# One level of Strassen's scheme in the MLP's up projection of a hybrid encoder layer (24 of 32 inner tiles), its results carried through DRAM

## The chip, the cores and the metric

The kernel runs on one core of a Trainium2 chip, in one launch. The metric is the device time of one execution in microseconds (us), from the first to the last instruction and what lies around them; the time stated for a kernel is the median of its runs. The core's engines run beside each other: TensorE (PE) multiplies, VectorE (DVE), ScalarE (ACT) and GpSimd (POOL) work element by element, SyncE (SP) issues every DMA of this kernel.

## The reference, cut to what matters

One layer of a streaming encoder, for 1024 prompt frames and 32 new frames that share the weights (1056 tokens, model width 1024, all float32). After a windowed attention, a short convolution and a memory cross attention comes the part that is changed:

```
hm = rms_norm(x, g_mlp)
x = x + jnp.square(jax.nn.relu(hm @ w_up)) @ w_down      # w_up 1024 x 4096, w_down 4096 x 1024
y = rms_norm(x, norm_final_g)
```

## The kernel before, in words

**Layout and precision.** Activations lie with features in the 128 partitions and tokens along the free axis. The tokens are cut into three chunks, `CH`: chunks 0 and 1 of 384 tokens, chunk 2 of 288. A width of 1024 is 8 feature tiles. Every operand of a large product is kept in two float32r parts, hi (a rounded copy, made by ACT) and lo (the rest, made by a subtraction), and `gemm` adds three matmuls for each of the 8 contraction tiles: hi by hi, hi weight by lo activation, lo weight by hi activation. One output tile of 128 features by one chunk is thus 24 matmuls of 384 or 288 columns, accumulated in one PSUM tile (`acc`, three buffers).

**Weights.** A weight tile is 128 by 1024: all 8 contraction tiles of 128 output features. `fetch_w` loads it (SP) into `wr` (two buffers), `issue_w` splits it into `wh` and `wl` (three buffers each). The split costs one ACT copy and one DVE subtraction; for the tiles that `shared` names (those of the phase with the cross attention) GpSimd makes the last 384 columns of `wl`. `next_w` keeps up to three tiles ready (`LOOK`).

**Order.** The program is a list, `plan`, of products with the weight tiles they need. From it a list scheduler fixes the order on each engine at build time: an instruction that is written later may stand earlier on its engine's queue where what it needs is ready by the scheduler's own clock. On the chip each queue runs in that fixed order.

**The phase around the change.** Chunk by chunk `trunk(c)` makes the convolution's output and the mixing product. The cross attention of chunk c, `cross_steps(c)`, is spread in 16 steps between the products of what follows: that of chunk 0 between those of `trunk(1)`, that of chunk 1 between those of `trunk(2)`, that of chunk 2 between the first products of the MLP. Its last steps are `do_co(c, 0)` and `do_co(c, 1)`, which add the result to the residual `x1[c][f]`, scale it by the norm's gain and split it into `xm[c][f]` (`gain_split`), and `chunk_stats(c)`, which makes the norm's factor `R[c]` for each token. The factor is not multiplied into `xm`; `up_part` multiplies the product by it.

**The MLP.** The 4096 inner features are 32 tiles j in four groups of 8. Group 0 goes up one chunk at a time (its 8 weight tiles are loaded three times), so that chunk 0 can start while chunk 2's attention is still at work. After that: `do_down` of group 0 (8 output tiles, three chunks each), `do_up` of group 1, `do_down` of group 1, and so on. `up_part` takes a PSUM tile through DVE (maximum with 0, times `R`), squares it on GpSimd and on ACT, and splits the square into `hid[c][j]`, which stays in SBUF (pools `mpool`, `hx`, `hpool`) for the down products. The last group goes down chunk by chunk (`do_last`), with the final norm of a chunk beside the next one's products.

Of the kernel before, what the change touches and what calls it, by code (L numbers as in the profile page):

```python
# [27 lines left out]
NHX = 6  # L28

# Columns of the parameter block.  # L30
# [9 lines left out]
def hybrid_step(ctx: ExitStack, tc: tile.TileContext, io):  # L40
# [38 lines left out]
    ao_d, bc_d, m1_d = spill("ao_d"), spill("bc_d"), spill("m1_d")  # L79
    mk_d = dram.tile([2, P, 256], F32, name="mk_d")  # L80
# [20 lines left out]

    LOOK = 2
    ready = []
# [34 lines left out]
    def next_w(key):  # L138
        while len(ready) <= LOOK and wpos[0] < len(worder):
            issue_w()  # L140
        k, w = ready.pop(0)
        assert k == key, (k, key)
        return w
# [6 lines left out]
    def gemm(out, w, acts):  # L150
        """out[m, n] = sum over k of w[k][:, m] . acts[k], operands in two parts."""
# [7 lines left out]
    def gemm_tok(a, ws, acts, cols):  # L159
        """a[tokens, 256] from a block of 128 tokens and a [1024, 256] weight in two tiles."""  # L160
# [8 lines left out]
    # ------------------------------------------------------------------ norms  # L169
# [4 lines left out]
    def stats_col(accs, blocks, rcol):  # L174
        """rcol[:, j] = rsqrt(mean + eps) of token block j, from partitions' sums of squares."""
# [14 lines left out]
    def stats_row(blocks, n, rcol):  # L190
        """rcol's values along the free axis, in every partition (in PSUM)."""
# [40 lines left out]
    # =========================================== input norm; memory keys, values  # L232
# [9 lines left out]
    def norm_x():  # L242
# [31 lines left out]
        def squares(c):  # L274
            """Two partial sums of squares, each on an engine of its own."""
# [92 lines left out]
    # ============================== phase 1: windowed attention, short convolution  # L368
# [13 lines left out]
    def vtile(src):  # L382
        """[v in two parts, per head] from float32 values."""
# [492 lines left out]
    def do_co(c, half):  # L876
        def fn(w):
# [3 lines left out]
            for f in fs:  # L881
# [9 lines left out]
                if half == 0:  # L891
                    xm[c][f] = gain_split(x, G_MLP + f, c)
# [11 lines left out]
    def hslot(c):  # L904
        n = CH[c][1]
        if c == 0:
            return mslot(n)
# [260 lines left out]
```

## Time and profile before

| | |
|---|---|
| runs before | 1844.49, 1844.90, 1846.09 us; median 1844.9 us |
| the profiled execution | span 1844.3 us from first to last instruction |
| instructions | 29362, of them 11508 matmuls |
| DMA | 163.26 MB, mean 89 GB/s |

The profile's page gives for each engine its busy time, the span in 40 slices, the chain of work that ended last, and groups of like instructions with their mean duration and the idle time before them. Busy times of matmuls overlap, since they are pipelined; how fast TensorE works is read from the distance between the starts of neighbouring matmuls in the timeline. Idle time of an engine counts only where TensorE waits for it.

### The profile page before, as it was taken

How to read it: one execution, taken by the hardware profiler on the slowest of the kernel's cores; microseconds unless marked ns; L12 is line 12 of the kernel's file. 1: busy time of each engine (PE TensorE's matmuls, PEld its weight loads, DVE VectorE, ACT ScalarE, POOL GpSimd, SP SyncE). 2: the span in 40 equal slices, each digit the busy share in tenths (PEclk: the TensorE clock that was granted, in tenths of full speed). 3: DMA queues.
4: the chain of work that ended last, by engine and by line, in shares of the span. 5: the costliest groups of instructions: out<-in, count | busy, mean ns of one | idle time of the engine just before them, and what ended most of it. 6: DMA issues, size and time to landing. Idle time of an engine off the chain costs nothing.

```text
span 1844.3 us, 29362 instructions
## 1 busy us (share of the span) xinstructions
PE 1816.0 (98%) x11508; PEld 1801.8 (98%) x11508; DVE 994.9 (54%) x1919; ACT 669.2 (36%) x1342; POOL 403.1 (22%) x441
## 2 busy tenths in 40 slices
PE   7999999999999999999999999999999999999997
PEld 7999999999999999999999899999999999999997
DVE  7766767757664223336788988622332233223355
ACT  7643435435344102324566766401210121012234
POOL 3211010201100000026656664400210021002132
PEclk9999999999999999999999999999999999999999
DMA  4411111212123124225444443411111111111244
GB/s 176 140 64 59 62 55 59 70 56 70 56 93 107 58 94 150 76 83 189 163 137 153 143 135 98 137 46 42 43 46 45 46 45 46 46 46 47 69 147 142
DMA packets 72747, 163.26 MB, mean 89 GB/s; under 512 B 8961, under 2 KB 41889, under 8 KB 72481
## 3 DMA queue, kind: packets, MB, share of 16 engines
q1 hardware_dynamic: 72608, 161.38, 26.7%
q8 instruction: 91, 1.49, 0.3%
q14 instruction: 48, 0.39, 0.1%
HBM read 142.66 MB, written 18.69 MB: 87 GB/s over the span
## 4 chain that ended last, share of the span: by engine, by line
PE 89%; DVE 3%; DMA 3%; issue 2%; ACT 2%; POOL 1%; SPq 0%; POOLq 0%; ACTq 0%; DVEq 0%
PE acc L155 27%; PE acc L156 27%; PE acc L157 27%; PE pt L524 1%; PE sc L499 1%; DVE wl L132 1%; PE sc L498 1%; PE o L537 1%; PE o L536 1%; ACT wh L130 1%; DMA ct<-m_d 1%; DMA mkr<-mk_d 1%; POOL wl L134 1%; PE acc L165 0%; DVE Y L230 0%
## 5 line engine op out<-in xcount | busy, mean ns | idle before, releaser
L130 ACT CAST wh<-wr 128x1024 fp32r<-128x1024 f32 x220 | 230.9, 1050 | 579.6 <-PE acc L156 508.7
L155 PE MATMUL acc<-X,wh 128*128 128x384 f32 (+1 forms) x1200 | 390.8, 326 | 8.5 <-ACT wh L130 8.0
L156 PE MATMUL acc<-X,wh 128*128 128x384 f32 (+1 forms) x1200 | 387.8, 323 | 2.4 <-DVE X L230 2.4
L155 PE MATMUL acc<-Y,wh 128*128 128x384 f32 (+1 forms) x1200 | 388.4, 324 | 0.5 <-DVE Ga L890 0.2
L156 PE MATMUL acc<-Y,wh 128*128 128x384 f32 (+1 forms) x1200 | 388.0, 323 | 0.0
L157 PE MATMUL acc<-Y,wl 128*128 128x384 f32 (+1 forms) x1200 | 387.6, 323 | 0.0
L157 PE MATMUL acc<-X,wl 128*128 128x384 f32 (+1 forms) x1200 | 386.8, 322 | 0.3 <-DVE wl L132 0.3
L132 DVE TENSOR_TENSOR wl<-wr,wh 128x1024 fp32r<-128x1024 f32 (+1 forms) x220 | 263.8, 1199 | 79.7 <-ACT wh L130 78.2
L155 PEld LDWEIGHTS acc<-X,wh 128*128 128x128 f32 x1200 | 226.3, 189 | 9.2 <-ACT wh L130 8.0
L156 PEld LDWEIGHTS acc<-X,wh 128*128 128x128 f32 x1200 | 226.5, 189 | 4.1 <-DVE X L230 3.6
L157 PEld LDWEIGHTS acc<-X,wl 128*128 128x128 f32 x1200 | 226.2, 189 | 0.8 <-DVE wl L132 0.8
L155 PEld LDWEIGHTS acc<-Y,wh 128*128 128x128 f32 x1200 | 225.3, 188 | 1.2 <-DVE Ga L890 0.4
L156 PEld LDWEIGHTS acc<-Y,wh 128*128 128x128 f32 x1200 | 225.2, 188 | 0.0
L157 PEld LDWEIGHTS acc<-Y,wl 128*128 128x128 f32 x1200 | 225.1, 188 | 0.0
L925 POOL TENSOR_TENSOR ct<-ct 128x384 f32<-128x384 f32 (+1 forms) x96 | 77.7, 810 | 542.0 <-DVE ct L923 535.8
L134 POOL TENSOR_TENSOR wl<-wr,wh 128x384 fp32r<-128x384 f32 x84 | 118.4, 1410 | 315.9 <-ACT wh L130 314.9
L155 PE MATMUL acc<-M,wh 128*128 128x384 f32 (+1 forms) x448 | 148.1, 331 | 1.7 <-ACT M L107 1.4
L156 PE MATMUL acc<-M,wh 128*128 128x384 f32 (+1 forms) x448 | 147.6, 329 | 0.0
L157 PE MATMUL acc<-M,wl 128*128 128x384 f32 (+1 forms) x448 | 147.4, 329 | 0.0
L155 PE MATMUL acc<-H,wh 128*128 128x288 f32 (+1 forms) x416 | 129.2, 311 | 0.0
L157 PE MATMUL acc<-H,wl 128*128 128x288 f32 (+1 forms) x416 | 128.9, 310 | 0.0
L156 PE MATMUL acc<-H,wh 128*128 128x288 f32 (+1 forms) x416 | 128.9, 310 | 0.0
(235 smaller groups left out, 2727.1 us busy)
## 6 DMA issues: line engine op xcount, KB each, us to landing
wr<-in_w_in SPq DMA_DIRECT2D x50, 512.0 KB, 3.3
wr<-in_w_up SPq DMA_DIRECT2D x48, 512.0 KB, 3.3
wr<-in_w_down SPq DMA_DIRECT2D x48, 512.0 KB, 3.4
wr<-in_w_conv_out SPq DMA_DIRECT2D x24, 512.0 KB, 3.4
wr<-in_w_mix SPq DMA_DIRECT2D x24, 512.0 KB, 3.4
ao_d<-AO SPq DMA_DIRECT2D x32, 128.0 KB, 1.8
wr<-in_w_attn_out SPq DMA_DIRECT2D x8, 512.0 KB, 3.3
raw<-in_x SPq DMA_DIRECT2D x8, 384.0 KB, 6.1
```

The source lines that it names most:

```text
L130: act.copy(hi, raw)
L132: dve.tensor_sub(lo[:, :cut], raw[:, :cut], hi[:, :cut].bitcast(F32))
L134: pool_e.tensor_tensor(lo[:, cut:], raw[:, cut:], hi[:, cut:].bitcast(F32), op=ALU.subtract)
L155: pe.matmul(out, wh[:, a], hi, start=(k == 0), stop=False)
L156: pe.matmul(out, wh[:, a], lo, start=False, stop=False)
L157: pe.matmul(out, wl[:, a], hi, start=False, stop=(k == len(acts) - 1))
L498: pe.matmul(sc[:, h, j * w : j * w + w], q[h], a, start=True, stop=False)
L499: pe.matmul(sc[:, h, j * w : j * w + w], q[h], b, start=False, stop=True)
L524: pe.transpose(pt[:, h * P : h * P + P], self.stl[:, h, t * P : t * P + P], ident)
L536: pe.matmul(of, v, ph, start=(t == 0), stop=False)
L537: pe.matmul(of, v, pl, start=False, stop=(t == len(self.parts) - 1))
L925: pool_e.tensor_tensor(s, t, t, op=ALU.mult)
```

## The change: what it does

A pair of inner tiles (ja, jb), the two halves of the contraction (tiles 0 to 3 and 4 to 7) and chunks 0 and 1 form a 2 by 2 block product: weights A11, A12 (tile ja, halves 1 and 2) and A21, A22 (tile jb), activations B11, B21 (chunk 0, the two halves) and B12, B22 (chunk 1). Written out it takes 8 block products of 12 matmuls; by one level of Strassen's scheme (Winograd's form) it takes 7, with sums of weights (`s31`, `s24`) and differences of activations (`N1`, `N3`, `T2`, `N4`) as operands and a few additions on the results. Groups 1 to 3 (24 tiles, 12 pairs) are done in this way; group 0 and all of chunk 2 stay written out.

- The two chunks must have their norm's factor before the differences are taken. `normed_split` multiplies `x1` by gain and `R`, stores the result to DRAM (`xn_d`) and splits it; it stands after `chunk_stats(c)`, and `do_co` no longer splits for chunks 0 and 1.
- `combine(k)` loads four tiles of `xn_d` back and makes and splits the four differences of contraction tile k. The four `combine` calls and the weights of the first pair stand between the 8 products of `up0(2)`, group 0 of chunk 2.
- All up products now come before all down products. A finished square goes to DRAM (`hid_d`) unsplit; `load_hidden` loads and splits it for the down products, one group ahead. Group 0 goes down chunk 0 first, then chunks 1 and 2, so that its 8 weight tiles are loaded twice.
- The pool `hx` is gone; `late`, which lives during the up products, holds 8 working tiles `lt`, the second weight tile of a pair and its sums.

```diff
@@ do_co
-                if half == 0:
+                if half == 0 and c == 2:
                     xm[c][f] = gain_split(x, G_MLP + f, c)
@@ the MLP's pieces
+    def normed_split(c, f):
+        t = tmp(CH[c][1])
+        dve.scalar_tensor_tensor(t, x1[c][f], col(G_MLP + f), R[c], op0=ALU.mult, op1=ALU.mult)
+        sp.dma_start(xn_d[c][:, f], t)
+        xm[c][f] = (yslot(c), yslot(c))
+        split(*xm[c][f], t)
     def up_part(w, c, j):
         n = CH[c][1]
-        a = acc_tile([P, n])
-        gemm(a, w, xm[c])
+        a = ps.tile([P, n], F32, tag="pt", bufs=2, name=nm("pa")) if w[0] == "late" else acc_tile([P, n])
+        gemm(a, w[-2:], xm[c])
         t = tmp(n)
-        dve.scalar_tensor_tensor(t, a, 0.0, R[c], op0=ALU.max, op1=ALU.mult)
-        s = tmp(n)
-        pool_e.tensor_tensor(s, t, t, op=ALU.mult)
-        hi, lo = hslot(c), hslot(c)
-        act.activation(hi, t, AF.Square)
-        dve.tensor_sub(lo, s, hi.bitcast(F32))
-        hid[c][j] = (hi, lo)
+        if c == 2:
+            dve.scalar_tensor_tensor(t, a, 0.0, R[c], op0=ALU.max, op1=ALU.mult)
+        else:
+            dve.tensor_scalar_max(t, a, 0.0)
+        h = tmp(n)
+        pool_e.tensor_tensor(h, t, t, op=ALU.mult)
+        hidden(c, j, h)
+    def combine(k):
+        b11, b12, b21, b22, n1, n3, t2, n4 = (lt() for _ in range(8))
+        for t, c, f in ((b12, 1, k), (b22, 1, k + 4), (b11, 0, k), (b21, 0, k + 4)):
+            sp.dma_start(t, xn_d[c][:, f])
+        dve.tensor_sub(n3, b12, b22)
+        pool_e.tensor_tensor(n1, b11, b12, op=ALU.subtract)
+        dve.tensor_sub(t2, b11, n3)
+        pool_e.tensor_tensor(n4, b21, t2, op=ALU.subtract)
+        for kind, x in (("T2", t2), ("N1", n1), ("N3", n3), ("N4", n4)):
+            hi, lo = comb[kind, k] = (comb_slot(kind, k), comb_slot(kind, k))
+            act.copy(hi, x)
+            if kind[0] == "T":
+                dve.tensor_sub(lo, x, hi.bitcast(F32))
+            else:
+                pool_e.tensor_tensor(lo, x, hi.bitcast(F32), op=ALU.subtract)
+    def pair_issue(key, which):
+        r1, r2 = raws[key][:2]
+        a, b = slice(0, 512), slice(512, 1024)
+        if which == 4:
+            s31 = L["pool"].tile([P, 1024], F32, tag="s31", name=nm("s31"))
+            s24 = L["pool"].tile([P, 1024], F32, tag="s24", name=nm("s24"))
+            pool_e.tensor_tensor(s31[:, b], r2[:, a], r2[:, b], op=ALU.add)
+            pool_e.tensor_tensor(s24[:, a], r1[:, a], s31[:, b], op=ALU.add)
+            pool_e.tensor_tensor(s24[:, b], r1[:, b], s24[:, a], op=ALU.add)
+            pool_e.tensor_tensor(s31[:, a], r1[:, a], r2[:, a], op=ALU.add)
+            raws[key] += [s31, s24]
...
+        split(hi, lo, raws[key][src])
+    def up_pair(i, after):
...
+        up_fetch(i + 1)
+        A, B, C = (acc_tile([P, 384]) for _ in range(3))
+        product(A, w(1), 0, b11, True)
+        s1 = lt()
+        act.copy(s1, A)
+        product(B, w(4), 0, t2, True)
+        u2 = lt()
+        dve.tensor_sub(u2, B, s1)
+        product(A, w(1), 1, b21, False)
+        r, h = lt(), lt()
+        act.activation(r, A, AF.Relu)
+        pool_e.tensor_tensor(h, r, r, op=ALU.mult)
+        hidden(0, ja, h)
+        product(C, w(3), 1, n1, True)
+        product(B, w(3), 0, n3, False)
+        u3 = lt()
+        dve.tensor_sub(u3, B, s1)
+        v = lt()
+        dve.tensor_sub(v, u3, C)
+        square_relu(v, 1, jb)
+        up_part(("late", *w(1)), 2, ja)
+        up_issue(i + 1, 1)
+        product(C, w(4), 1, b22, False)
+        up_issue(i + 1, 4)
+        v = lt()
+        dve.tensor_sub(v, C, u2)
+        square_relu(v, 1, ja)
+        product(B, w(2), 1, n4, False)
+        up_issue(i + 1, 3)
+        v = lt()
+        dve.tensor_sub(v, B, s1)
+        square_relu(v, 0, jb)
+        up_part(("late", *w(2)), 2, jb)
+        up_issue(i + 1, 2)
+    def load_hidden(into, g, c, k):
+        t = tmp(n)
+        sp.dma_start(t, hid_d[c][:, 8 * g + k])
...
+        split(hi, lo, t)
@@ the order
-    left = beside(left + cross_steps(2), up0(0) + up0(1) + up0(2))
+    left = beside(left + cross_steps(2), up0(0) + up0(1))
+    for j in range(NF):
+        item(*do_up(j, 2))
+        if j < 4:
+            item(lambda j=j: combine(j))
+        if j == 4:
+            item(lambda: up_fetch(0))
+        if j == 5:
+            item(lambda: up_issue(0, 1))
+        if j == 6:
+            item(lambda: [up_issue(0, 4), up_issue(0, 2)])
+    item(lambda: up_issue(0, 3))
+    for i in range(len(UP)):
+        item(lambda i=i: up_pair(i, first_loads if i == len(UP) - 1 else lambda what: None))
+    item(open_down)
+    item(lambda: [load_hidden(nxt, 0, c, k) for c in (1, 2) for k in range(NF)])
-    for g in range(4):
-        if g:
-            for j in range(NF):
-                item(*do_up(g, j, range(3)))
-        if g < 3:
+    for g in range(3):
+        item(turn_group)
+        for cs, more in (([0], []), ([1, 2], range(3))) if g == 0 else ((range(3), range(3)),):
             for f in range(NF):
-                item(do_down(f), ("w_down", g, f))
+                item(do_down(g, f, cs, more), ("w_down", g, f))
```

In this diff `hidden(c, j, h)` stores `h` to `hid_d[c]`; `product` is 12 matmuls (4 contraction tiles, 3 each); `which` 1, 2, 3, 4 stands for the tiles `r1`, `r2` (split into `wh2`, `wl2`), `s31` and `s24`; `square_relu` makes max(v, 0) times v on DVE and stores it. In the last pair `first_loads` loads and splits group 0 of chunk 0 as the first two products free their operands' places.

More of the change, by code (lines that the diff above doesn't have):

```diff
@@ new lines, in product @@
+    def product(acc, w, half, acts, start):
+        wh, wl = w
+        for k, (hi, lo) in enumerate(acts):
+            a = slice(512 * half + k * P, 512 * half + k * P + P)
+            pe.matmul(acc, wh[:, a], hi, start=(start and k == 0), stop=False, skip_group_check=True)
+            pe.matmul(acc, wh[:, a], lo, start=False, stop=False, skip_group_check=True)
+            pe.matmul(acc, wl[:, a], hi, start=False, stop=(k == 3), skip_group_check=True)
+    UP = [(8 * g + i, 8 * g + i + 4) for g in range(1, 4) for i in range(4)]
@@ L969, in cross_steps @@
         steps.append(("call", [lambda: chunk_stats(c)]))
+        if c < 2:
+            steps[-1][1].extend(lambda f=f: normed_split(c, f) for f in range(NF))
         return steps
@@ L987, in trunk @@
         ]
-    up0 = lambda c: [do_up(0, j, [c]) for j in range(NF)]
+    up0 = lambda c: [do_up(j, c) for j in range(NF)]
     first = len(worder)
```

113 lines of the change are left out of this document (86 added, 27 removed).

## The prediction

> **What bounds the kernel now.** I read the page first: the busy shares and the chain of work that ended last.
>
> ```profile
> span 1844.3 us, 29362 instructions
> ## 1 busy us (share of the span) xinstructions
> PE 1816.0 (98%) x11508; PEld 1801.8 (98%) x11508; DVE 994.9 (54%) x1919; ACT 669.2 (36%) x1342; POOL 403.1 (22%) x441
> ...
> PE 89%; DVE 3%; DMA 3%; issue 2%; ACT 2%; POOL 1%; SPq 0%; POOLq 0%; ACTq 0%; DVEq 0%
> ```
>
> TensorE is busy 98% of the span and is 89% of the chain, so taking matmuls away should take time away, unless their place is filled by waiting. Whether it is filled is a question of stages, so I cut the stretch that the change touches into windows. In each row: length, then busy time of PE, weight loads, DVE, ACT, POOL.
>
> ```profile
> 945.00:985.00 40.00, 39.12 (x236) 37.95 (x235) 36.05 (x47) 25.39 (x40) 33.34 (x27) 1.00 0.38 128
> 985.00:1045.00 60.00, 58.97 (x424) 58.01 (x423) 53.12 (x101) 38.79 (x83) 33.20 (x30) 1.00 0.50 165
> 1045.00:1060.00 15.00, 12.96 (x79) 11.80 (x78) 13.48 (x19) 11.09 (x20) 13.39 (x13) 1.00 0.36 118
> 1060.00:1157.60 97.60, 96.01 (x608) 95.10 (x608) 84.94 (x146) 59.92 (x128) 56.64 (x48) 1.00 0.36 117
> 1157.60:1183.30 25.70, 25.61 (x193) 25.37 (x192) 20.00 (x35) 13.16 (x21) 15.12 (x14) 1.00 0.49 162
> 1183.30:1831.00 647.70, 647.70 (x4036) 647.70 (x4035) 227.43 (x346) 123.13 (x183) 83.79 (x93) 1.00 0.19 62
> ```
>
> The first three rows are cross attention of chunks 0 and 1, the fourth that of chunk 2 beside `up0(0)` and `up0(1)`, the fifth `up0(2)`, the last the rest of the MLP. In the last TensorE is never idle and DVE is at 227 of 648 us: room for everything. In the rows before it DVE runs at 78 to 90% and TensorE already loses a little (2.0 us in the third row). So the gain is made where there is room, and the preparation is put where there is little.
>
> **The gain.** The price of a matmul is the distance of starts, here across one output tile of 384 columns and one of 288:
>
> ```profile
> 1186.21 0.33 PE L157 MATMUL acc<-M,wl 128*128 128x384 f32 x1
> ...
> 1190.54 0.29 PE L155 MATMUL acc<-H,wh 128*128 128x288 f32 x1
> ...
> 1193.74 0.34 PE L155 MATMUL acc<-M,wh 128*128 128x384 f32 x1
> ```
>
> There are 25 steps of 384 columns in 4.33 us, 0.1732 us each, and 24 of 288 in 3.20 us, 0.1333 each. A pair took 2 tiles x 2 chunks x 24 = 96 matmuls of 384 columns and takes 7 x 12 = 84; chunk 2's 48 stay. 12 pairs x 12 = 144 matmuls, x 0.1732 = **24.9 us gained**. A pair lasts 84 x 0.1732 + 48 x 0.1333 = 20.9 us, a product of 12 lasts 2.1 us, a tile of chunk 2 lasts 3.2 us.
>
> **Inside the pairs.** These rows price what is added:
>
> ```profile
> L130 ACT CAST wh<-wr 128x1024 fp32r<-128x1024 f32 x220 | 230.9, 1050 | 579.6 <-PE acc L156 508.7 <-issue 45.1 <-DMA wr<-in_w_down 7.1
> L132 DVE TENSOR_TENSOR wl<-wr,wh 128x1024 fp32r<-128x1024 f32 x2 | 2.5, 1271 | 2.0 <-ACT wh L130 2.0
> L938 DVE TENSOR_TENSOR Gb<-acc,Gb 128x384 f32<-128x384 f32 x40 | 22.3, 557 | 97.5 <-PE acc L157 97.5
> L923 DVE SCALAR_TENSOR_TENSOR ct<-acc,R 128x288 f32<-128x288 f32 x8 | 3.4, 447 | 0.0
> L226 POOL TENSOR_TENSOR xacc<-xacc,ct 128x384 f32<-128x384 f32 x4 | 5.3, 1316 | 0.2
> L925 POOL TENSOR_TENSOR ct<-ct 128x288 f32<-128x288 f32 x7 | 5.4, 778 | 5.2 <-DVE ct L923 5.2
> ```
>
> GpSimd: four weight sums of 512 columns, by the two-input row of 384 1.316 x 4/3 = 1.76 each, one square of 384 and two of 288: 7.0 + 1.3 + 1.6 = 9.9 us of 20.9. DVE: four `wl` (5.1), eight steps on results (8 x 0.557 = 4.5, more where both inputs lie in SBUF), two of chunk 2 (2 x 0.447): 10.5. ACT: four `wh` and two copies, about 5.2. All fit. A result is awaited by the next product into its PSUM tile: u2 has two products' time (4.2 us), the two steps on C have the 3.2 us of chunk 2's tile against 1.1 and perhaps one `wl` ahead of them (1.3). I cost the steady pairs at nothing; the price if the cover goes is the second rival.
>
> **Through DRAM.** 16 stores of `xn_d`, 16 loads, 96 stores and 96 loads of squares, 8 more weight loads, and on SP an issue each:
>
> ```profile
> L121 SPq DMA_DIRECT2D wr<-in_w_up x48: 327/328/334, 1050.0 to 1682.6; - x48
> m_d<-ct SPq DMA_DIRECT2D x16, 192.0 KB, 1.8
> ct<-bc_d SPq DMA_DIRECT2D x16, 192.0 KB, 3.6
> ```
>
> 232 x 0.33 = 77 us of SP in some 800. In the first pass of group 0 down (8 x 24 x 0.1732 = 33.3 us) it has most to move: 8 weights of 512 KB, 8 tiles of 192 and 8 of 144, 6.9 MB or 207 GB/s: more than the 162 of the row of `up0(2)`, well below the 367 of a row shown further down. The splits move, their number doesn't change (96 before and after, in the window with 420 us of DVE to spare). The group's first 8 tiles are loaded behind the first two products of the last pair and have 16 us for 3.6 us of landing and 8 x 0.56 of DVE. I cost all this at 0; if the loads came only after the pair, the wait would be about 8 us.
>
> **Chunks 0 and 1 normed before the split.** `gain_split` took one DVE instruction for each tile, `normed_split` takes two, and 8 of them come as a block:
>
> ```profile
> L230 DVE SCALAR_TENSOR_TENSOR Y<-Gb,prm,Y 128x384 fp32r<-128x384 f32 x20 | 23.4, 1172 | 0.0
> L108 DVE TENSOR_TENSOR Y<-ct,Y 128x384 fp32r<-128x384 f32 x32 | 16.7, 552 | 6.7 <-ACT Y L107 6.5
> ```
>
> For chunk 0, 8 x 1.17 = 9.4 us leave the row 945 to 985 and 8 x (0.56 to 1.17 + 0.55) = 9 to 14 us enter the row 985 to 1045, where DVE has 60 - 53.1 = 6.9 free. The weights' `wl` are queued behind them on DVE, one each 3.2 us in `trunk(2)`, and three ready tiles cover 9.6 us. So 2 to 7 us are late, less what the earlier row gives up: I take 3, bounds 0 and 7. For chunk 1 the block moves out of the row that loses 2.0 us into `up0(0)`, where the splits of squares go: a gain, I take 2. Together **+1**.
>
> **The change-over at `up0(2)`.** Here lies the cost. What GpSimd does in that window now, one group that DVE does there, and the stretch before:
>
> ```profile
> L134 POOL TENSOR_TENSOR wl<-wr,wh 128x384 fp32r<-128x384 f32 x6 | 8.6, 1426 | 3.4 <-ACT wh L130 2.3 <-PE acc L155 1.0
> ...
> L925 POOL TENSOR_TENSOR ct<-ct 128x384 f32<-128x384 f32 x1 | 1.3, 1342 | 1.3 <-DVE ct L923 1.3
> ...
> L928 DVE TENSOR_TENSOR H<-ct,H 128x288 fp32r<-128x288 f32 x7 | 6.0, 864 | 0.6 <-POOL ct L925 0.6
> ...
> 1138.50:1157.60 19.10, 17.51 (x112) 16.60 (x111) 18.90 (x27) 13.16 (x25) 14.39 (x13) 1.00 0.31 105
> ...
> 1159.55 1.01 POOL L134 TENSOR_TENSOR wl<-wr,wh 128x384 fp32r<-128x384 f32 x1
> 1162.29 1.65 POOL L134 TENSOR_TENSOR wl<-wr,wh 128x384 fp32r<-128x384 f32 x1 [1.74 <-ACT wh L130]
> ```
>
> 8.6 + 5.4 + 1.3 = 15.3 us of 25.7. To it come 4 x 5 = 20 instructions of `combine` (two differences, three lo parts), then three sums before `s24` can be split. The same instruction of 384 columns took 1.01 and 1.65 us; I take 1.316, the mean of the row with DVE busy. 15.3 + 20 x 1.316 + 3 x 1.76 = 46.9 us; perhaps 3 of them can run before 1157.6 (from 1138.5, when the cross attention's tiles come free, POOL is idle for 4.7 us; DVE, which must go first, for 0.2). So `s24` is there at 43.9 us of the stage, its split (1.05 + 1.27) at 46.2. TensorE asks for it after 25.7 + 2.1 = 27.8 us: 18 us late in the order as written. But the scheduler doesn't keep that order where something else is ready:
>
> ```profile
> 1135.19 0.34 PE L156 MATMUL acc<-Y,wh 128*128 128x384 f32 x1
> 1135.37 0.28 PE L859 MATMUL o<-PTh,mv 128*128 128x256 f32 x1
> 1135.48 0.34 PE L157 MATMUL acc<-Y,wl 128*128 128x384 f32 x1
> ```
>
> Here attention matmuls stand inside another product. Without `s24` the pair has a second product on A (2.1) and both tiles of chunk 2 (6.4) to put forward: 18.4 - 8.5 = **9.9 us of waiting**. Bounds: at 1.01 for each instruction and 4.7 us early, 15.3 + 20.2 + 4.0 - 4.7 + 2.3 - 27.8 - 8.5 = 1 us is left; at 1.65, none early and the order as written, 15.3 + 33 + 6.6 + 2.3 - 27.8 = 29.
>
> A wait of that length also costs clock, as the start of this run shows (granted clock in the third column from the end):
>
> ```profile
> 12.00:16.00 4.00, 1.79 (x7) 0.95 (x6) 4.00 (x4) 3.35 (x6) 3.84 (x5) 1.00 1.00 333
> 16.00:20.00 4.00, 3.78 (x16) 3.79 (x17) 4.00 (x5) 1.63 (x3) 1.02 (x1) 0.57 1.01 367
> ```
>
> After 2.2 us of idling the next 4 us ran at 0.57: 4 x 0.43 = **1.7 us**.
>
> **The sum** against the profiled execution: 1844.3 - 24.9 + 1.0 + 9.9 + 1.7 = 1832.0. The median of the runs lies 0.6 above that span: **1832.6 us**.
>
> **Rivals.**
> 1. *The change-over is hidden.* The scheduler starts `combine` early and GpSimd's prices are near 1.01. For it: POOL is idle 42% of the row 1060 to 1157.6. Against it: the working tiles are late and DVE is full there. 1832.6 - 9.9 - 1.7 = 1821; with chunk 0's block costing its upper bound, 1825.
> 2. *The sums are late in every pair; slower than before.* `up_issue(i + 1, 4)` is written after C's second product. If POOL's queue keeps it there, behind chunk 2's square, the chain from the end of that tile is 0.45 + 0.78 + 3 x 1.76 + 1.05 + 1.27 = 8.8 us, with two steps of 0.56 to 1.2 ahead of it on DVE 10 to 11, against a cover of 2.1 + 2.1 + 3.2 + 2.1 = 9.5. At 1.65-prices (2.2 for a sum) it is 12. Late by 0.5 to 2.5, say 2.0: 12 x 2.0 = 24 us, 1857. It decides from 1.3 us a pair: 12 x 1.3 = 15.6 is what the forecast leaves below 1844.9 plus the 3.7 of a real difference. For it: the margin is small; against: the sums wait for nothing but loads made 20 us before, and the scheduler moved other work forward.
> 3. *GpSimd at its upper price.* With DVE as full as POOL in the change-over (20.0 of 25.7 us now; 6.0 of splits go, 12 instructions of `combine` at 0.55 to 1.17 come), each of the 23 instructions may take 1.65 or 2.20 instead of 1.316 or 1.76: 20 x 0.334 + 3 x 0.44 = 8 us more, 1840.6. For it: the window's six L134 average 1.43 already; against: 1.01 is met there too. The Trainium skill's page "SBUF — State Buffer", section "Who interferes with whom", states it as a rule: a DVE instruction with two SBUF inputs and a GpSimd instruction that reads SBUF exclude each other for their whole length. By that rule `combine` speaks against itself, as it feeds both engines at once, and this rival's time holds; the two prices in the rows agree with it.
> 4. *DVE binds in the front.* Both blocks hit a full DVE: 7 for chunk 0, nothing back for chunk 1, and the lo parts of `combine` pushed behind: 1832.6 + 6 to 12, about 1842. For it: rows of 88 to 90% DVE; against: 9.4 us leave the row before.
>
> That it doesn't do what it says would show as a matmul count other than 11508 - 144 = 11364; nothing in the diff suggests it.
>
> **How the numbers follow.** Forecast 43% (its own range 1826 to 1841); rival 1 25%; rival 2 15%; rival 3 9%; rival 4 8%. The range reaches over the forecast and rivals 1, 3 and 4 and leaves out most of rival 2: 1819 to 1850. A measurement of this kernel can tell about 0.2% (3.7 us) from no change. Faster by more: 43 + 25 + 5 of rival 3 + 2 of rival 4 = 75%. Within: 4 of rival 3, 5 of rival 4, 1 of rival 2, 10%. Slower: 14 of rival 2, 1 of rival 4, 15%.
>
> **What would show it.** 11364 matmuls and a stretch of pairs of 20.9 us each: gain right; longer pairs: rival 2, with TensorE waiting for `wh` or `wl` of `s24`. One gap of 5 to 15 us between `up0(2)` and the second product, POOL without a pause before it and the clock below 1.00 behind it: the change-over right; no gap: rival 1. A gap near 20 us with GpSimd's instructions at 1.65: rival 3. TensorE idle between 985 and 1060 more than the 3.1 us of now: rival 4. I'd be wrong in another way if loads of `hid_d` held up the first down products, or if SP's queue stood behind a `combine` load that waits for a working tile while a weight load waits behind it.

## The result, and the profile after

| | before | after |
|---|---|---|
| runs (us) | 1844.34, 1844.49, 1844.90, 1846.09 | 1864.91, 1865.72, 1868.00, 1868.33 |
| median | 1844.7 | 1866.9 |
| ratio after to before | | 1.0117, 95% interval 1.0103 to 1.0131 |
| the profiled execution's span | 1844.3 | 1863.1 |

The change makes the kernel slower by 1.2%; the forecast was 1832.6 and its range ended at 1850. These are the first lines of the page of after:

```profile
span 1863.1 us, 29794 instructions
## 1 busy us (share of the span) xinstructions
PE 1801.2 (97%) x11364; PEld 1785.5 (96%) x11364; DVE 1074.3 (58%) x2027; ACT 719.5 (39%) x1414; POOL 469.3 (25%) x473
```

The 144 matmuls are gone (11508 - 144 = 11364). So time was won, and more was lost elsewhere. The profiled execution of after is the fastest of its four, so the spans differ by 18.8 us where the medians differ by 22.2; what follows explains the 18.8. The same stretch as in the prediction, cut into windows (length; then busy time of PE, weight loads, DVE, ACT, POOL; then the granted clock, the DMA's share and GB/s):

```profile
980.00:1005.00 25.00, 15.74 (x96) 15.53 (x95) 18.81 (x44) 13.40 (x25) 9.54 (x8) 0.80 0.51 165
1005.00:1040.00 35.00, 34.83 (x259) 34.53 (x259) 29.70 (x52) 22.79 (x51) 16.96 (x15) 1.00 0.40 140
1040.00:1075.00 35.00, 33.23 (x223) 32.15 (x222) 27.12 (x44) 21.87 (x39) 30.66 (x29) 1.00 0.47 160
1075.00:1105.00 30.00, 21.63 (x124) 21.30 (x125) 22.67 (x48) 13.49 (x27) 10.13 (x8) 0.83 0.45 158
1105.00:1150.00 45.00, 45.00 (x286) 45.00 (x285) 32.89 (x61) 23.73 (x59) 20.37 (x18) 1.00 0.42 148
1150.00:1170.00 20.00, 16.94 (x104) 16.47 (x103) 16.40 (x22) 11.38 (x22) 13.70 (x12) 0.98 0.73 257
1170.00:1190.00 20.00, 15.94 (x99) 14.88 (x97) 19.20 (x21) 9.61 (x18) 20.00 (x16) 0.94 0.41 126
1190.00:1210.00 20.00, 6.39 (x26) 5.46 (x27) 12.25 (x17) 7.34 (x13) 18.43 (x19) 0.57 0.39 131
1210.00:1230.00 20.00, 20.00 (x134) 20.00 (x134) 9.06 (x10) 5.64 (x6) 10.43 (x11) 0.91 0.51 165
...
1250.00:1460.00 210.00, 210.00 (x1322) 210.00 (x1321) 107.22 (x141) 51.91 (x61) 82.98 (x69) 1.00 0.31 103
1460.00:1830.00 370.00, 370.00 (x2282) 370.00 (x2281) 166.13 (x264) 105.62 (x172) 23.14 (x17) 1.00 0.38 126
```

The last two rows are the pairs and the down products: TensorE is never idle there. Everything lost lies before, in three places: about 980 to 1000, 1083 to 1092 and 1160 to 1213. Length minus PE's busy time, added up from 980 to 1230, is 40.3 us; the rows of before from 985 to 1183.3 gave 4.8.

How much was won and how much lost is read from where the first pair begins. In the timeline of TensorE the last tile of `up0(2)` ends and the pair's product goes on at

```profile
1226.64 0.29 PE L160 MATMUL acc<-Y,wl 128*128 128x288 f32 x1
1226.77 0.34 PE L1002 MATMUL acc<-Y,wl 128*128 128x384 f32 x1
```

Four of the pair's matmuls (0.6 us) had been put forward, so the pairs' share begins at 1226.2. In before the last matmul of `up0(2)` and the first of the down products stand at

```profile
1182.06 0.30 PE L157 MATMUL acc<-Y,wl 128*128 128x288 f32 x1
1182.20 0.33 PE L155 MATMUL acc<-M,wh 128*128 128x384 f32 x1
```

so `up0(2)` ended at 1182.2, about 1 us before the end of the prediction's fifth row (1183.3). From there to the end of the span it was 1844.3 - 1182.2 = 662.1 us and is now 1863.1 - 1226.2 = 636.9: **25.2 us won**. Up to there it takes 1226.2 - 1182.2 = **44.0 us more**: 35.5 of idling, and 8.5 that is left for the lower clock. 44.0 - 25.2 = 18.8, the difference of the spans.

The waits of TensorE in after from 940 to 1240 (total, times, longest) name the three places:

```profile
PE acc L158 <- DVE ct L735: 9.3, 1, 9.3
PE acc L158 <- DVE ct L933: 8.4, 1, 8.4
PE pq L183 <- POOL xacc L229: 7.6, 1, 7.6
PE pr L201 <- ACT ct L199: 4.9, 1, 4.9
PE acc L888 <- DVE ct L933: 2.8, 1, 2.8
```

**First and second place: a block in DVE's queue.** The first line waits for an evacuation of `do_conv_out` (L735), the second for one of `up_part` (L933). DVE's timeline at the first (start, duration, operation; "x3" are three in a row):

```profile
977.35 0.56 DVE L750 TENSOR_TENSOR Gb<-acc,ct 128x384 f32<-128x384 f32 x1 [1.43 <-PE acc L160]
...
989.40 2.40 DVE L917 SCALAR_TENSOR_TENSOR ct<-Ga,prm,R 128x384 f32<-128x384 f32 x3
...
997.32 0.44 DVE L735 TENSOR_TENSOR ct<-acc,Ga 128x288 f32<-128x288 f32 x1
```

Between the evacuation at 977.35 and the next at 997.32 no `acc` tile is emptied. TensorE fills three tiles of 288 columns (from 977.15, 3.2 us each, with the norm's small matmuls between) and stops at about 988. `normed_split` stands ahead of the evacuations, since the scheduler fixed that order; it needs `R[0]`, which ACT writes from 988.56 to 989.04, so DVE first sits through the norm's chain, then works off the block, then empties the tile that was full at 980.5. In before the same evacuation stands inside the norm's chain, between its instructions, and there is no block behind it:

```profile
987.70 0.45 DVE L733 TENSOR_TENSOR ct<-acc,Ga 128x288 f32<-128x288 f32 x1
```

**Third place: GpSimd's queue.** Its timeline shows `combine` (L963 here, L954 and L956 soon after) between the additions of chunk 2's sum of squares (L229):

```profile
1169.28 1.77 POOL L229 TENSOR_TENSOR xacc<-xacc,ct 128x288 f32<-128x288 f32 x1
1171.01 1.04 POOL L935 TENSOR_TENSOR ct<-ct 128x384 f32<-128x384 f32 x1
1172.02 1.33 POOL L963 TENSOR_TENSOR M<-lt,M 128x384 fp32r<-128x384 f32 x1
1173.30 1.60 POOL L963 TENSOR_TENSOR hx<-lt,hx 128x384 fp32r<-128x384 f32 x1
...
1197.81 1.11 POOL L229 TENSOR_TENSOR xacc<-xacc,ct 128x288 f32<-128x288 f32 x1
```

The last addition starts at 1197.81; the norm's factor of chunk 2 is written at

```profile
1206.48 0.40 ACT L212 COPY R<-pr 128x288 f32<-128x288 f32 x1 [1.27 <-PE pr L202]
```

Until then no tile of `up0(2)` can be evacuated, since `up_part` multiplies by `R[2]`. In before this factor was written at 1165.08. POOL is busy 20.00 of 20 and 18.43 of 20 us from 1170 to 1210. Of the 20.7 us that TensorE idles from 1150 to 1230, 13.5 are waits for the chain that makes `R[2]` (7.6, 4.9 and 1.0); evacuations and `wl` make up most of the rest. The sums of weights, on which the forecast let TensorE wait, come later and hold up nothing.

### The profile page after: what moved, and what is told of

Its sections match the earlier page's. It is cut to its first block, busy times and chain, and to the rows that moved or that the text cites. A ratio compares the mean times of both kernels' runs of the same rounds, so it can differ in the third digit from the quotient of the medians.

```text
span 1863.1 us, 29794 instructions
## 1 busy us (share of the span) xinstructions
PE 1801.2 (97%) x11364; PEld 1785.5 (96%) x11364; DVE 1074.3 (58%) x2027; ACT 719.5 (39%) x1414; POOL 469.3 (25%) x473
## 3 DMA queue, kind: packets, MB, share of 16 engines
q8 instruction: 90, 1.47, 0.3%
## 5 line engine op out<-in xcount | busy, mean ns | idle before, releaser
L158 PE MATMUL acc<-Y,wh 128*128 128x384 f32 (+1 forms) x1008 | 329.5, 327 | 18.6 <-DVE ct L735 9.3
L160 PE MATMUL acc<-Y,wl 128*128 128x384 f32 (+1 forms) x1008 | 328.9, 326 | 4.2 <-DVE wl L135 2.7
L159 PE MATMUL acc<-Y,wh 128*128 128x384 f32 (+1 forms) x1008 | 328.8, 326 | 0.0
L158 PEld LDWEIGHTS acc<-Y,wh 128*128 128x128 f32 x1008 | 192.3, 191 | 19.5 <-DVE ct L735 9.5
L160 PEld LDWEIGHTS acc<-Y,wl 128*128 128x128 f32 x1008 | 191.9, 190 | 4.9 <-DVE wl L135 3.2
L159 PEld LDWEIGHTS acc<-Y,wh 128*128 128x128 f32 x1008 | 192.0, 190 | 0.0
L229 POOL TENSOR_TENSOR xacc<-xacc,ct 128x384 f32<-128x384 f32 (+1 forms) x62 | 73.7, 1190 | 344.1 <-ACT ct L227 343.1
L158 PE MATMUL acc<-M,wh 128*128 128x384 f32 (+1 forms) x320 | 105.0, 329 | 0.3 <-DVE Gb L892 0.2
L159 PE MATMUL acc<-M,wh 128*128 128x384 f32 (+1 forms) x320 | 104.6, 327 | 0.2 <-DVE M L111 0.2
L160 PE MATMUL acc<-M,wl 128*128 128x384 f32 (+1 forms) x320 | 104.5, 326 | 0.0
L1090 DVE TENSOR_TENSOR Gb<-acc,Gb 128x384 f32<-128x384 f32 (+1 forms) x60 | 31.4, 523 | 112.6 <-PE acc L160 112.6
L110 ACT CAST PTh<-pt 128x512 fp32r<-128x512 f32 (+3 forms) x94 | 46.0, 517 | 123.3 <-PE pt L527 122.4
L158 PE MATMUL acc<-H,wh 128*128 128x288 f32 (+1 forms) x256 | 80.7, 315 | 0.0
```

The source lines that it names most:

```text
L110: act.copy(hi, src)
L158: pe.matmul(out, wh[:, a], hi, start=(k == 0), stop=False)
L159: pe.matmul(out, wh[:, a], lo, start=False, stop=False)
L160: pe.matmul(out, wl[:, a], hi, start=False, stop=(k == len(acts) - 1))
L229: pool_e.tensor_tensor(acc, acc, sq, op=ALU.add)
L1090: dve.tensor_add(x, a, x)
```

## The experiments

Times are of one execution unless an interval is given; before on the same chips took 1844.9 us beside the first eight runs and 1845.9 beside x10. "Windows" are the rows of busy time as above.

One thing must be taken out first. ACT writes a norm's factor at about 900 us, ahead of everything that the change touches, and already this row differs by up to 3.4 us between executions:

```profile
899.45 0.48 ACT L212 COPY R<-pr 128x384 f32<-128x384 f32 x1
902.85 0.48 ACT L212 COPY R<-pr 128x384 f32<-128x384 f32 x1
```

The first is x8's, the second x10's. So parts of a few us are compared by what comes after this row, the span less its start:

| | before | after | x1 | x2 | x3 | x4 | x5 | x6 | x7 | x8 | x10 |
|---|---|---|---|---|---|---|---|---|---|---|---|
| the row's start | 901.8 | 901.0 | 902.1 | 901.9 | 901.3 | 902.5 | 900.6 | 901.7 | 902.9 | 899.5 | 902.9 |
| span less start | 942.5 | 962.1 | 952.5 | 960.7 | 950.3 | 950.4 | 951.4 | 949.9 | 955.1 | 926.9 | 947.5 |
| above before | | 19.6 | 10.0 | 18.2 | 7.8 | 7.9 | 8.9 | 7.4 | 12.6 | -15.6 | 5.0 |

Counted from this row, after's loss ahead of the first pair is (1226.2 - 901.0) - (1182.2 - 901.8) = 44.8 us, and 44.8 - 25.2 = 19.6. How far the later stretches differ from one execution to the next was not measured apart, so differences of about 1 us in this table carry nothing.

### What each part costs: x8 and x10

The first takes both preparations away and lets the pairs stand. What it computes for chunks 0 and 1 is not the layer any more, since the factor and the differences are left out; it is there for its time alone.

```diff
@@ do_co, cross_steps: gain_split for all chunks, no normed_split
-                if half == 0 and c == 2:
+                if half == 0:
@@ combine(k)
+        comb["T2", k] = xm[0][k]
+        for kind in ("N1", "N3", "N4"):
+            comb[kind, k] = xm[1][k]
```

> The changed kernel without the two preparations: do_co splits all three chunks as before (without the norm's factor, which then is left out of chunks 0 and 1), normed_split and combine are gone, and tiles of xm stand in for T2, N1, N3, N4. The pairs, their weight sums and the way through DRAM stay. Theory: pairs and DRAM cost what was predicted (24.9 us gained, nothing lost), all the loss is in the preparations: 1819 to 1824 us. Rival: the pairs' GpSimd work or the loads of hid_d cost time too: above 1828 us.

It took 1828.4 us (span 1826.4). Its windows:

```profile
980.00:1005.00 25.00, 25.00 (x176) 25.00 (x176) 20.08 (x40) 13.90 (x25) 13.99 (x12) 1.00 0.48 156
1150.00:1170.00 20.00, 17.86 (x121) 17.62 (x120) 10.63 (x21) 9.12 (x15) 13.79 (x13) 0.93 0.56 177
1170.00:1190.00 20.00, 17.70 (x114) 17.23 (x114) 8.07 (x10) 5.04 (x5) 11.05 (x10) 0.89 0.43 149
```

The first two places are gone (TensorE is also busy 30.00 of 30 us from 1075 to 1105). At the change-over 4.4 us of idling and some clock stay, with neither DVE nor POOL full. TensorE's largest waits from 1150 to 1190 are

```profile
PE acc L158 <- DVE ct L931: 2.1, 1, 2.1
PE acc L158 <- ACT wh L133: 2.0, 1, 2.0
```

The first is for an evacuation of `up0(2)`, which needs `R[2]` (written at 1164.81). The second is for the last weight tile of `up0(2)` itself: SP issues its load only at 1176.48, behind loads for the first pair, and ACT waits 9.4 us for it. Here `up0(2)` ends at 1188.6 with 0.6 us of the first pair put forward, so by the count above (1188.0 - 899.5) - 280.4 = 8.1 us are lost ahead of the pairs, 4.4 by idling and 3.7 left for the clock. The pairs and all behind them take 1826.4 - 1188.0 = 638.4 us, 1.5 more than in after, with TensorE never idle from 1190 to 1800; why is open. By the table, 25.2 - 15.6 = 9.6 us are lost in all. The time lies on the rival's side (above 1828), but not for the rival's reason: neither the pairs' GpSimd work nor the loads of `hid_d` stop TensorE. So the pairs and the way through DRAM bring what was forecast for them to within 1.5 us, and the change-over costs something even without a preparation.

The second run has `normed_split` as the change has it, and still no `combine`.

> The changed kernel with its normed_split where it stands, but combine makes nothing: normed tiles stand in for T2, N1, N3 and N4, so the outputs of chunks 0 and 1 are not the reference's. Theory (two separate losses): the waits at 980 to 1000 and 1083 to 1092 stay, about 18 us and some clock, on top of the 1828.4 of the run without either: 1845 to 1851, and the change-over idles no more than in that run (about 5 us of 60). Rival (the two losses are one backlog, so that the late normed_split also makes the change-over late): the change-over idles over 10 us, 1853 or more.

1852.2 us (span 1850.4), between the two figures: by the time nearer the rival's 1853, by the idling nearer the theory. The first two places are back as in after (8.4 us of idling from 1075 to 1105), and the change-over idles 6.8 us from 1150 to 1210, against 4.4; the two waits of x8 are among them (2.1 and 2.4):

```profile
980.00:1005.00 25.00, 15.75 (x97) 15.54 (x97) 20.04 (x44) 12.98 (x26) 11.07 (x9) 0.74 0.55 184
```

So the 44.8 us divide into 9.6 that is lost with neither preparation, 947.5 - 926.9 = **20.6 for `normed_split`** and 962.1 - 947.5 = **14.6 for `combine`**. Counted only up to the first pair (1211.7 in x10) they are 8.1, 20.3 and 16.4. These are of one execution each, and each part was taken away in one order only; x6 below shows that the parts do not simply add.

### The block: x1, x2, x5

In x1 one `normed_split` follows each of the next 8 products, in place of 8 in a block.

```diff
-        if c < 2:
-            steps[-1][1].extend(lambda f=f: normed_split(c, f) for f in range(NF))
+    def normed_beside(c, fillers):
+        ...
+            out.append((lambda w, fn=fn, f=f: (fn(w), normed_split(c, f) if f < NF else None), key))
```

> The changed kernel with one edit: normed_split is called once behind each of the 8 products that follow (trunk(2) for chunk 0, up0(0) for chunk 1), not 8 times in a block. Theory: the block of 16 DVE instructions and the 8 ct tiles it takes stand in front of the PSUM evacuations; TensorE's waits of 9.3 us (980 to 1000) and 8.4 us (1080 to 1100) fall below 2 us each and the clock stays at 1.00 there: 1842 to 1850 us. Rival: DVE is short of time in these stretches whatever the order; the waits come elsewhere in them and the time stays above 1858 us.

1856.6 us. Its windows:

```profile
1005.00:1040.00 35.00, 31.35 (x233) 30.11 (x233) 34.03 (x59) 21.39 (x51) 15.48 (x15) 1.00 0.51 169
1040.00:1075.00 35.00, 28.82 (x164) 26.40 (x163) 27.19 (x40) 19.66 (x35) 26.20 (x24) 0.90 0.33 112
```

The time lies in neither range (1842 to 1850, above 1858). The wait of 9.3 us is gone (24.91 of 25 from 980 to 1005, and no idling at the second place). But DVE is now busy 34.03 of 35 us in `trunk(2)`, and TensorE idles 9.8 us there, which it did not in after (1.9): the waits moved, as the rival said, at half of the price. The change-over idles 20.6 us as before. By the table x1 stands 10.0 us above before, after 19.6. A block hurts by its place; without it the work itself hurts, as DVE has little room for it.

In x2 the values of `normed_split` get six places of their own, so that they cannot hold up a user of the shared ring `ct`.

```diff
-        t = tmp(CH[c][1])
+        t = cr.tile([P, 384], F32, tag="ns", bufs=6, name=nm("ns"))
```

> The changed kernel with one edit: normed_split's t has six places of its own (in the cross attention's pool) instead of the shared six of ct; the 8 calls stay one block. Theory A, the ct ring: evacuations get their place and go ahead of the block, both waits fall below 3 us each, 1846 to 1853 us. Theory B, the DVE queue: the block still stands in front of the evacuations, the waits stay at 7 us or more each, 1860 to 1867 us.

1864.6 us, as after (1.4 us better by the table). The evacuation does go ahead of the block now, as theory A said: it stands inside the norm's chain again,

```profile
985.80 0.45 DVE L735 TENSOR_TENSOR ct<-acc,Ga 128x288 f32<-128x288 f32 x1
```

where in after it came at 997.32. So the ring did set that order. But the time is theory B's, because the block then holds up something else in DVE's queue, the next norm's statistic (L188 at 995.67, L191 at 1003.25). TensorE's largest entry from 940 to 1240 is

```profile
PE pr L201 <- ACT ct L199: 18.5, 3, 6.6
```

with 6.6 us at 1004.47, just under theory B's 7; 6.4 of the 18.5 belong to the change-over. Freeing one user of the queue from the block puts the next one in its place.

In x5 chunk 0's eight are spread over all 16 products of `trunk(2)`, and their two factors are put in by ACT (the gain) and GpSimd (`R`); chunk 1's stand as in x1.

```diff
+        if c == 0:
+            act.mul(t, x1[c][f], col(G_MLP + f))
+            pool_e.tensor_tensor(t, t, R[c], op=ALU.mult)
```

> normed_split spread as in x1_spread, but chunk 0's over all 16 products of trunk(2) and its product with R made by ACT and GpSimd instead of DVE. In x1_spread TensorE waited 10 us between 1005 and 1075 with DVE at 34.0 of 35 us. If that was DVE's shortage, 8 instructions fewer there bring the waits in 980 to 1075 below 4 us and the time to 1848 to 1852 us; if it was something else (the order, the added loads), it stays at 1854 or more.

1853.7 us, between the two ranges, and by the table only 1.1 better than x1: half the density, and still 7.6 us of idling from 1005 to 1075 (TensorE busy 31.93 of 35 and 30.43 of 35 us), against less than 4 expected. So DVE's shortage was part of x1's idling there; what the rest waits for stays open.

### The change-over: x3, x4, x7

In x3 `combine` has no GpSimd instruction: `b12` and `b21` stand in for `N1` and `N4`, and all use the lo part of `T2`. So it does not compute the layer either; `combine`'s loads, DVE's and ACT's work stay.

> The changed kernel without combine's five GpSimd instructions: N1 and N4 are not formed (b12 and b21 stand in) and N1, N3, N4 use the lo part of T2; loads, DVE's and ACT's work stay. Theory: GpSimd's backlog in the change-over makes the 20 us of TensorE waiting between 1160 and 1220; it falls below 6 us, 1845 to 1851 us. Rival: DVE's fullness or the loads through the eight lt places make it; at least 14 us stay, 1859 us or more.

1853.4 us, in neither range (1845 to 1851, 1859 or more). Its windows:

```profile
1170.00:1190.00 20.00, 16.09 (x104) 14.77 (x103) 18.06 (x29) 12.98 (x26) 13.23 (x11) 0.99 0.65 215
1190.00:1210.00 20.00, 15.78 (x101) 15.31 (x102) 5.73 (x10) 4.79 (x6) 12.04 (x12) 0.84 0.48 150
```

Idling from 1150 to 1230 falls from 20.7 to 10.1 us, with DVE still at 18.06 of 20 in the first row. Of what is left, 6.8 us are there without any `combine` (x10).

In x4 `combine` keeps its instructions, but all are queued behind the last addition for `R[2]`.

```diff
+            last_add[c] = pool_e.tensor_tensor(acc, acc, sq, op=ALU.add)
...
+        with tc.issue_after(getattr(ins, "ins", ins)):
+            combine(k)
```

> The changed kernel with one edit: combine's GpSimd instructions are queued behind the last addition to chunk 2's sum of squares; no work is taken away. If the order alone is at fault (R of chunk 2 comes late, its adds wait behind combine), the waiting of 20 us between 1160 and 1220 falls below 6 us, 1845 to 1851 us. If the amount of GpSimd work is at fault, R comes some 25 us earlier but TensorE then waits for the first pair's operands instead: 8 to 16 us of waiting stay, 1854 to 1863 us.

1854.6 us: as much as x3 by the table (7.9 and 7.8 above before), by order alone. Idling from 1150 to 1230 is 11.4 us. `combine` adds 20.7 - 6.8 = 13.9 us of idling, of which order alone takes away 9.3, two thirds; of its 14.6 us it gives back 11.7. The time lies in the range of the other case, that the amount of work is at fault, but the waits that are left are not for the first pair's operands, as that case had it: they are for evacuations (3.4 us) and for the norm's chain of chunk 2 (2.8 and 2.8). `R[2]` is written at 1196.08, 10 us earlier than in after and not 25, and 17 us after the last addition, since the chain's small DVE instructions now run beside `combine`'s.

In x7 `combine` is cut in two: `N1` and `N3` beside `up0(1)`, `T2` and `N4` at the old place behind the last addition.

> normed_split as in the changed kernel (a block). combine is cut in two: N1 and N3 are made beside up0(1), where GpSimd is at 20 of 45 us, and n3 goes through DRAM; T2 and N4 are made beside up0(2), their GpSimd instructions (8 instead of 20) queued behind the last addition to chunk 2's sum of squares. lt has 7 places instead of 8. Theory (GpSimd's amount and order together): waits between 1150 and 1230 fall from 20 to below 7 us, 1848 to 1853 us. Rival (DVE's fullness in do_co of chunk 2, which stays): 12 us or more remain, 1857 or more.

1860.2 us, on the rival's side by time (1857 or more), with 10.4 us of idling at the change-over between the two cases (below 7, 12 or more), about as in x4. But 1.7 us more are idle from 1075 to 1105, 2.0 from 1105 to 1150 and 1.5 after 1300, so by the table it is 7.0 better than after and 4.7 worse than x4: taking work out of the change-over put some of the loss elsewhere.

### Both together: x6

x6 is x5 and x7 in one.

> x5_spread16 and x7_splitonly together, t of normed_split in lt. If the two losses are separate and additive: 1832 to 1838 us, faster than before. If the relief in one place only moves the backlog of DVE and GpSimd to the other: 1842 or more.

1853.4 us, by the table 1.5 better than x5 alone, so the expectation of 1832 to 1838 failed and its rival (1842 or more) held. Part of the miss was known before, since x5 and x7 had each brought less than hoped; but 10.7 us regained by x5 and 7.0 by x7 make 17.7, and together they regain 12.2. The idling is spread over the whole front, the stretch ahead of the first pair: 3.2, 2.8, 1.6, 5.5, 1.9, 2.3, 3.7 and 4.5 us in the eight windows from 980 to 1210 that are shown above for after. Relief at one place moves part of the backlog to the next; the front could not take the work in any order that was tried.

### Elsewhere: x9, x11, x12

If the front has no room, the preparation can come later. In all three runs group 1 is written out too (8 pairs, so 2/3 of 25.2, 16.8 us, to win), with `gain_split` and `R` at the evacuation as before the change.

In x9 `normed_split(0, j)` stands beside group 1's products of chunk 1, `normed_split(1, j)` beside group 0's of chunk 2, `combine` beside group 1's of chunk 2.

> Group 1 is written out too (8 pairs instead of 12), with unnormed operands and the factor R at the evacuation for groups 0 and 1, as before the change; normed_split of chunk 0 stands beside group 1's products of chunk 1, that of chunk 1 beside group 0's products of chunk 2, combine beside group 1's products of chunk 2. The gain left is 8 x 12 x 0.1732 = 16.6 us of 1844.9, so 1828.3 if nothing waits. Theory (the loss is DVE and GpSimd work put into a stretch where both are full): the waits at 980 to 1105 and 1160 to 1213 go, 1827 to 1833. Rival (the preparation of the pairs costs its time wherever it stands, because DVE and GpSimd slow each other or SP's loads come late): over 1838.

1844.1 us, ratio 0.9988 (0.9979 to 0.9998), 0.1% below before and on the rival's side (over 1838): the front is well again, but the stretch with `combine` loses 7.1 us of idling from 1240 to 1300, and clock (0.91 and 0.83). What happens there shows in the groups of DVE by line, the first from 1240 to 1250, the second from 1252 to 1280, when `combine`'s instructions are on GpSimd:

```profile
L135 DVE TENSOR_TENSOR wl<-wr,wh 128x1024 fp32r<-128x1024 f32 x3 | 3.7, 1226 | 3.1 <-ACT wh L133 3.1
```

```profile
L135 DVE TENSOR_TENSOR wl<-wr,wh 128x1024 fp32r<-128x1024 f32 x6 | 10.3, 1721 | 1.2 <-ACT wh L133 1.2
```

The same split of a weight takes 1.226 us and 1.721. This slowing explains half of the 7.1 us at most: 3.5 of them end at such a `wl`, and another 3.5 at a `wh` whose weight came late (ACT waits 6.5 us for the DMA there). The rival had named both.

x11 spreads it: chunk 1's values beside group 1's products of chunk 0, the four `combine` some 13 us apart.

> As the run with group 1 written out too, but the preparation is thinned further: chunk 1's normed values are made and stored beside group 1's products of chunk 0, the four combine calls stand about 13 us apart over group 0's and group 1's products of chunk 2 (51 us in place of 25). In that run TensorE idled 7.1 us of 1240 to 1300 and lost about 5 us to the clock, waiting for wh and wl, with VectorE's instructions at up to twice their length beside GpSimd's. Theory (what counts is how many of combine's instructions fall into each microsecond, since the two engines slow each other): that stretch loses under 2 us, 1829 to 1835. Rival (the work costs the same wherever it is spread): 1841 to 1846.

1846.7 us, ratio 1.0006 (0.9997 to 1.0016), no difference from before, and just above the rival's 1841 to 1846. TensorE's largest wait from 1180 to 1300 is

```profile
PE acc L160 <- DVE wl L135: 6.2, 6, 2.3
```

and 3.7 us more end at `wh`. Weight tiles are due every 3.2 us there. From 1215 to 1300 ACT waits 24.2 us for weights that land late, and SP, which issues them in a fixed order with stores and loads, waits 26.8 us for GpSimd's squares before stores. This is akin to the case of SP's queue that the prediction had named as a way to be wrong, but it is a store that SP stands at, not a load of `combine`. In after no wait of TensorE from 940 to 1240 ends at a `wh` of ACT.

x12 puts the values and `combine` where one weight tile serves two chunks (8.3 us), and leaves only 16 loads and splits for the stretch of chunk 2:

```diff
+    for j in range(NF):
+        item(lambda w, j=j: [up_part(w, c, NF + j) for c in range(2)], ("w_up", NF + j))
+        if j < 4:
+            item(lambda j=j: [normed(c, f) for f in (j, j + 4) for c in (1, 0)])
+        if j in (1, 3, 4, 6):
+            item(lambda j=j: combine({1: 0, 3: 1, 4: 2, 6: 3}[j]))
```

> As the two runs with group 1 written out, but the preparation stands where a weight tile serves two chunks: group 1 goes up with chunks 0 and 1 for each weight (8.3 us of TensorE a weight tile, 66 us), and beside it stand the normed values of both chunks and the four combine calls (T2 and N4 of the last two contraction tiles go to DRAM unsplit); over the 16 products of chunk 2 that follow (3.2 us a weight tile) only 16 tiles are loaded and split, without GpSimd. In the run before this one, TensorE idled 10 us of 1220 to 1300 for wl and wh, while weights were due each 3.2 us and SP issued them behind stores and loads that waited. Theory (the preparation hurts where a weight tile is due each 3 to 4 us, and not where one is due each 8 us): 1829 to 1836. Rival (it costs its time anywhere): 1840 to 1847.

1841.0 us against 1846.2 on its chip, ratio 0.9970 (0.9954 to 0.9985): 0.3% below before, the most of any version, but not within the theory's 1829 to 1836; it lies in the rival's range of 1840 to 1847. Its largest waits from 1170 to 1300 are

```profile
PE acc L159 <- DVE ct L935: 3.3, 2, 1.7
PE acc L161 <- DVE wl L136: 2.0, 3, 1.0
```

All waits there come to 7.0 us, against 9.9 in x11. The first line's two waits (at 1198.33 and 1208.53) lie in the roomy stretch itself. Room helps, but of 16.8 us only 3.4 are left by the spans (1844.3 - 1840.9), and 5.2 by the medians. Whether a stretch with still longer weight tiles, such as the down products, would take the work for nothing was not tried.

## Why the prediction was wrong, point by point

**The gain, and the pairs: right.** 24.9 us forecast, 25.2 measured, 11364 matmuls, TensorE busy 210.00 of 210 us in the pairs. Rival 2 (sums late in every pair) did not occur.

**Through DRAM: right.** Nothing was costed, and the row 1460 to 1830 shows no idling.

**"Chunks 0 and 1 normed before the split", +1: this is the step that failed most; it cost 20.6.** The step compared DVE's added time with its free time in the row, and let only the weights' `wl` be late behind it. What stood behind it were the evacuations of PSUM. TensorE has three `acc` tiles, 9.6 us of chunk 2's products, and the block plus the norm's chain ahead of it kept DVE from evacuating for 20 us (977.35 to 997.32). And the 2 us given back for chunk 1 were a loss too: the same block stopped TensorE for 8.4 us at 1083. A block that waits for a late result is priced by the time in which nothing behind it runs, not by its busy time. DVE's free time counts as well, since x1 idles 9.8 us in `trunk(2)` with no block; the reckoned upper bound for chunk 0 was 7. The sign of rival 4 came true (11.0 us of idling from 985 to 1060, against 3.1); its place was right, its size not.

**The change-over, 9.9 + 1.7: right resource, wrong wait, too small.** GpSimd was the bottleneck, as said, and its prices were not what failed: the twenty instructions of `combine` took 0.98 to 1.60 us, 1.20 in the mean (1.316 assumed), a weight sum 1.27 to 1.47 (1.76 assumed). But the wait was reckoned at `s24`, behind all of `combine`, with `up0(2)` as its cover. The scheduler put `combine` ahead of the additions for `R[2]`, so that the cover itself could not run: the gaps came in `up0(2)`, and none between it and the second product, where the forecast had its sign. The prediction knew that the scheduler moves work forward and used it only in favour (8.5 us of cover). In place of 11.6 us, 8.1 are lost ahead of the pairs even without `combine` (x8), a term that the sum did not have, and `combine` costs 14.6 over the whole run. x4 shows that order is the larger part of `combine`'s cost: without a single instruction less, it gives back 9.3 of 13.9 us of idling.

**The clock: right in kind, its price somewhat low.** 8.5 us beside 35.5 of idling, 0.24 for each (9.3 and 0.26 from the common row); the forecast had 1.7 for 9.9, 0.17.

**Rivals and range.** Rival 1 (hidden) was wrong. Rival 3 (GpSimd at 1.65) was not needed: the mean price was 1.20. Rival 4 had the first place, but with 6 to 12 us in all, where the two blocks cost 20.6. The range ended at 1850, and no choice among the prediction's own bounds reaches the result. With the block at 7 and nothing back for chunk 1 (6 more) and the change-over at 29 for 9.9 with the clock in proportion (about 22 more), an estimate from its own terms is about 1861; all runs lie above 1864. What was missing were the waits themselves, not only their coincidence.

## What to carry to other kernels

Before work is added in a stretch where an engine is at 80 to 90%, list what stands behind it in that engine's queue, PSUM evacuations and the norm's statistic first: the price is the time that those are held up less the tiles that cover it, and part of it is paid again in clock. A saving of matmuls whose operands need preparing is worth what is left after a place for the preparation is found; here 25 us were won and no place tried took the preparation for less than about 12 (x12: 16.8 to win, 5.2 left). Small parts of a run are compared from a row that the change doesn't touch: by the spans alone `normed_split` would have seemed to cost 24.0 us in place of 20.6. An estimate of queue order that helps the forecast must be tried the other way round as well.

## What the runs showed of the hardware that was not expected

An instruction of DVE on three elements a partition can take 0.9 us. In the norm's chain of chunk 2 in after, with an instruction of GpSimd beside it:

```profile
1201.36 0.99 POOL L137 TENSOR_TENSOR wl<-wr,wh 128x384 fp32r<-128x384 f32 x1
1201.45 0.92 DVE L189 TENSOR_TENSOR st_t<-st_t,st_y 128x3 f32<-128x3 f32 x1
```

and in x3, where `combine` leaves GpSimd alone:

```profile
L189 DVE TENSOR_TENSOR st_t<-st_t,st_y 128x3 f32<-128x3 f32 x1 | 0.2, 161 | 0.0
```

The long one ends at 1202.37, the GpSimd instruction at 1202.35; its neighbours end in the same way, L188 at 1201.41 beside one that ends at 1201.40, and L191 (0.91 us) at 1204.27 beside one that ends at 1204.25. The Trainium skill's page "SBUF — State Buffer", section "Who interferes with whom", says that a DVE instruction with two SBUF inputs and a GpSimd instruction that reads SBUF lock each other out; these rows and the 1.226 and 1.721 us of `wl` in x9 agree. So in these rows a small DVE instruction lasted as long as what was left of the GpSimd instruction beside it, and a chain of four (L188 to L191) took 3.2 us, against 0.8 in the chain at 983 in the same run.

The granted clock fell to 0.57 in a window with 13.6 us of idling and was still 0.91 in the 20 us after it, in which TensorE was never idle.
